# A second column chunk by seven products in a decoder trunk's feed-forward blocks, with two of four weight sums made by accumulating DMA

## The chip, the cores and the metric

The kernel runs on one core of a Trainium2 chip. The metric is the time of one execution in microseconds of device time. The median of three executions of the kernel before is 1845.34 us (1844.8 to 1848.62).

## What is computed

Four decoder layers on 256 tokens of width 1024, all in float32. Each layer has a feed-forward block, a mixer (a short gated convolution, a latent attention, a spatial gating, then the convolution again) and another feed-forward block. The change touches the feed-forward blocks only:

```python
def swiglu(x, w_gate, w_up, w_down):          # w_gate, w_up: 1024 x 2816, w_down: 2816 x 1024
    return (jax.nn.silu(x @ w_gate) * (x @ w_up)) @ w_down

x = x + 0.5 * swiglu(rms_norm(x, norm_g[i, 0]), ffn_gate[i, 0], ffn_up[i, 0], ffn_down[i, 0])
```

There are eight such blocks. The first one is computed plainly in both kernels, so what follows happens seven times.

## The kernel before, in words

**Tiling.** The 256 tokens are two tiles of 128 (t = 0 and t = 1). A float32 product is made of three passes: operand and weight are each split into a high part (`hi`, rounded to the type that TensorE reads) and the rest (`lo`), and hi*hi, hi*lo and lo*hi are added up in PSUM. ScalarE (ACT) makes the high part of a weight unit of 128 x 1024 elements (line 111, tile `whi`), VectorE (DVE) subtracts it from the raw weights (line 122, tile `wlo`), and both token tiles use the pair. The columns of gate and up are cut into chunks of 512 (`FF_CHUNKS`; chunk 5 has 256).

**Turns.** Each token tile is a Python generator (`stream`, `ffn`); one step of it is a turn, which issues about six matmuls with one weight unit (`products`, lines 332, 333, 335). The two tiles take turns alternately (`advance`). The schedule is manual: every engine executes its instructions in the order in which the program issued them.

**Seven products.** For the chunks in `SEVENS` the gate and up products of both token tiles together are computed as a 2 x 2 block product, with the token tiles as the block rows and 256 columns as a block column. Seven block products stand in for eight (Winograd's form of Strassen's scheme). This is the generator `sevens`. It first makes token sums s1 to s4 (the set-up). Then, for each of its units (gate and up of each chunk), it goes through seven products q = 0 to 6. A product is 12 matmuls of 256 columns (line 773 before). Its right operand is one of four weight blocks "11", "12", "21", "22" of 128 x 1024 elements, or a sum of two of them:

```python
right = ("11", "11", "11", "21", "12", "11", "22")
added = (None, "12", "22", None, "22", "21", None)
```

So q = 1, 2, 4 and 5 each need a sum, made in place by DVE (`sum_of`, line 655). Every product's operand goes through `high_of` (ACT, line 631) and `low` (DVE, line 636). Each product is two half-steps of the generator: the first issues drains of earlier products, the next `low` and sums; the second issues the matmuls and the `high_of` two products ahead.

**Order of work.** `beside` decides when the generator moves: at each turn it adds `RATE` half-steps of credit (0.6) and spends whole ones. `block_of` (line 599) loads a block on SP's DMA queue; `load_first` loads the first four during the mixer, and `load` the next unit's four during q = 3, 4 and 5. There are four block buffers, whose names rotate (`next_buffers`): the next unit's "11" goes where "21" was, its "12" where "11" was, its "22" where "12" was, its "21" where "22" was. In the lane of seven products a buffer is thus loaded again when its last `low` is done.

Of the kernel before, what the change touches and what calls it, by code (L numbers as in the profile page):

```python
# [18 lines left out]
ALU = mybir.AluOpType  # L19
# [27 lines left out]
CHAIN_AHEAD = 3  # L47
LAG = 4
CLOSE_AT, CLOSE_LAG = 10, 1
H_READ, H_TAKE, SEVENS_READ = 7, 2, 7  # L50
SEVENS, RATE = (4,), 0.6
SEVENS_TAIL = 10
DOWN_TAIL, OUT_TAIL = 12, 4
X_TURN, X_WRITE, X_READ, X_TAKE = 2, 1, 3, 12
# [112 lines left out]
def program(nc, pools, order, x, positions, norm_g, ffn_gate, ffn_up, ffn_down,  # L167
# [5 lines left out]
    def name(tag):  # L173
        ids[0] += 1
        return f"{tag}_{ids[0]}"

    def slot(shape, dtype=F32):
        return slots.tile(shape, dtype, tag="s", name=name("s"))
# [4 lines left out]
    def acc():  # L183
        return banks.tile([P, 512], F32, tag="bank", name=name("acc"))
# [30 lines left out]
    pause = [0] * NT  # L215
    lag = [LAG]
    lanes = []
    credit = [0.0]
    own = [0] * NT

    def unit(t, m, k, n, c0, width):
# [367 lines left out]
    def next_buffers():  # L589

        buffers.update({"11": buffers["21"], "12": buffers["11"], "22": buffers["12"], "21": buffers["22"]})

    def block_of(i, j, n, m, name_):

        row, col = int(name_[0]) - 1, int(name_[1]) - 1
        c0 = FF_CHUNKS[n][0] + 256 * col
        view = matrices[m][i, j].rearrange("(kt p) n -> p kt n", p=P)[:, 4 * row : 4 * row + 4, c0 : c0 + 256]
        raw = sevens_pool.tile([P, 4, 256], F32, tag=f"block{buffers[name_]}", name=name("block"))
        nc.sync.dma_start(out=raw, in_=view)
        return raw  # L600

    def load_first(i, j, every):
# [8 lines left out]
    def sevens(i, j, chunks, shared, first):  # L611

        (a11, a12), (a21, a22) = lhs[0], lhs[1]
        units = [(n, m) for n in chunks for m in ("gate", "up")]
        raws = [first] + [{} for _ in units[1:]]

        def load(u, *names):
            for name_ in names:
                if u < len(units):
                    raws[u][name_] = block_of(i, j, *units[u], name_)  # L620
# [3 lines left out]
        def combine(x, y, op):  # L624
            f = slot([P, 4, P])
            nc.vector.tensor_tensor(out=f, in0=x, in1=y, op=op)
            return f

        def high(key, src, pool, shape):
            hi, lo = (pool.tile(shape, F32R, tag=tag, name=name(tag)) for tag in ("whi", "wlo")) if pool else (slot(shape, F32R), slot(shape, F32R))  # L630
            nc.scalar.activation(hi, src, AF.Copy)  # L631
            forms[key] = hi, lo, src

        def low(key):
            hi, lo, src = forms[key]
            nc.vector.tensor_tensor(out=lo, in0=src, in1=hi.bitcast(F32), op=ALU.subtract)  # L636
# [3 lines left out]
        def form(key, x, y, op):  # L640
            forms_of_x[key] = combine(x, y, op)
            return forms_of_x[key]

        def high_x(key):
            high(key, forms_of_x[key], None, [P, 4, P])

        right = ("11", "11", "11", "21", "12", "11", "22")
        added = (None, "12", "22", None, "22", "21", None)
        last = 7 * len(units) - 1

        def sum_of(s):
            u, q = divmod(s, 7)
            if s <= last and added[q]:
                to = raws[u][right[q]]
                nc.vector.tensor_tensor(out=to, in0=to, in1=raws[u][added[q]], op=ALU.add)  # L655

        def high_of(s):
            if s <= last:
                high(s, raws[s // 7][right[s % 7]], w_pool, [P, 4, 256])

        s1 = form("s1", a21[2], a22[2], ALU.subtract)
        yield
        s2 = form("s2", s1, a11[2], ALU.subtract)
        high_x("s1")
        high_of(0)
        yield
        low("s1")
        form("s3", a11[2], a21[2], ALU.subtract)
        high_x("s2")
        yield  # L670
        low(0)
        sum_of(1)
        high_x("s3")
        yield
        low("s2")
# [1 line left out]
        high_of(1)  # L677
        yield

        pending = []  # L680
        y = z = x = None
        gates = [None, None]
# [2 lines left out]
        def snapshot(ps):  # L685
            v = slot([P, 256])
            nc.scalar.activation(v, ps[:, :256], AF.Copy)
            return v

        def add(to, ps, v, op):  # L690
            nc.vector.tensor_tensor(out=to, in0=ps[:, :256], in1=v, op=op)
# [42 lines left out]
        for s in range(last + 1):  # L734
            u, q = divmod(s, 7)

            if q == 1:
                v1 = snapshot(y)
            elif q == 3:
                v2 = snapshot(y)  # L740
            elif q == 4:
                vs = [slot([P, 512]) for _ in range(NT)]
                add(vs[0][:, :256], x, v1, ALU.add)
            elif q == 5:
                v3 = snapshot(y)
            elif q == 6:
                add(vs[1][:, 256:], z, v3, ALU.subtract)
            if s + 1 <= last:
                low(s + 1)
            if (s + 2) % 7 in (1, 2):  # L750
                sum_of(s + 2)
            if q == 3:
                next_buffers()
                load(u + 1, "11")
            if q == 4:
                load(u + 1, "12", "22")
            if q == 5:
                load(u + 1, "21")
            if pending:
                pending.pop(0)()  # L760
            yield
            if q == 0:
                y = acc()
            elif q == 1:
                z = acc()
            elif q == 3:
                x = acc()
            ps = (y, z, y, x, y, y, z)[q]
            left = (a11, forms["s1"], forms.get("s2"), a12, forms.get("s3"), a22, forms.get("s4"))
            ah, al, wh, wl = left[q][0], left[q][1], forms[s][0], forms[s][1]  # L770
            for k in range(4):
                for n, (f, w) in enumerate(((ah, wh), (ah, wl), (al, wh))):
                    nc.tensor.matmul(ps[:, :256], lhsT=f[:, k, :], rhs=w[:, k, :], start=q in (0, 1, 3) and k + n == 0, stop=k == 3 and n == 2,  # L773
                                     skip_group_check=True)
            del forms[s]
            high_of(s + 2)
            if (s + 3) % 7 in (4, 5):
                sum_of(s + 3)
            if s == 0:
                low("s3")  # L780
                high_x("s4")
            if s == 1:
                low("s4")
            if q == 6:
                if u % 2 == 0:
                    pending += gate_halves(y, z, v2, vs)
                else:
                    pending += up_halves(y, z, v2, vs, chunks[u // 2], lambda: gates)
            yield
# [494 lines left out]
    def beside():  # L1284
        if not all(half_ is not None for tile_ in lhs for half_ in tile_):
            return
        credit[0] += RATE
        while lanes and credit[0] >= 1:
            credit[0] -= 1
            if next(lanes[0], "end") == "end":  # L1290
                lanes.pop()
                credit[0] = 0.0

    for _ in range(LAG):
        advance(0)
# [33 lines left out]
```

## Time and profile before

| what | value |
|---|---|
| median of three executions | 1845.34 us |
| the profiled execution's own time | 1846.8 us |
| its span, first to last instruction | 1845.1 us |
| instructions | 24822 |
| PE (TensorE matmuls) busy | 1821.9 us, 99% |
| DVE busy | 1286.7 us, 70% |
| ACT busy | 989.3 us, 54% |
| POOL (GpSimd) busy | 146.6 us, 8% |
| HBM read and written | 365.67 MB and 33.03 MB |

The profile comes from one execution. Busy time is the union of an engine's instructions. Matmuls overlap each other by design, so what one costs is read from the distance of two starts and not from its own duration. A DMA's time is counted from its issue to the landing of its last byte.

### The profile page before, as it was taken

The page shows a single profiled execution, that of the slowest core. Times are in us where ns is not written, and L with a number is a line of the kernel's source. Part 1 is how long each engine was busy: PE and PEld are TensorE (multiplying, and loading weights), DVE is VectorE, ACT ScalarE, POOL GpSimd, SP SyncE. Part 2 cuts the span into 40 slices and gives each one's busy share as a digit, 9 for nine tenths or more (in the row PEclk, how much of TensorE's full clock was granted, in tenths as well). Part 3 has the DMA queues.
Part 4 walks back from the last instruction along what each step waited for, and adds up shares of the span by engine and source line. Part 5 has one row for each costly group of instructions (what it writes and reads, how often), then busy time and mean ns, then how long its engine had stood idle before and what let it go on. Part 6 is the DMA issues. An engine that isn't in the chain of part 4 may idle for free.

```text
span 1845.1 us, 24822 instructions
## 1 busy us (share of the span) xinstructions
PE 1821.9 (99%) x9022; PEld 1516.7 (82%) x9022; DVE 1286.7 (70%) x1574; ACT 989.3 (54%) x1422; POOL 146.6 (8%) x279
## 2 busy tenths in 40 slices
PE   8999999999999989999999999999999999999999
PEld 6888887888788868888878888888887888878887
DVE  5556677877687666687668665678667775777773
ACT  5344545554555476554565446565456555546542
POOL 2000101000430142100010001100000000000000
PEclk9999999999999999999999999999999999999999
DMA  7678666669666842676977786657886777665774
GB/s 264 212 244 229 227 213 209 208 195 298 224 217 193 250 154 70 194 226 196 267 238 226 217 262 213 217 176 229 240 262 205 226 233 231 236 204 184 226 235 130
DMA packets 251610, 400.35 MB, mean 217 GB/s; under 512 B 25414, under 2 KB 116448, under 8 KB 251488
## 3 DMA queue, kind: packets, MB, share of 16 engines
q1 hardware_dynamic: 250480, 397.09, 68.7%
q8 instruction: 70, 1.15, 0.3%
q0 software_dynamic: 608, 1.11, 0.2%
q10 hardware_dynamic: 400, 0.57, 0.1%
q14 instruction: 52, 0.43, 0.1%
HBM read 365.67 MB, written 33.03 MB: 216 GB/s over the span
## 4 chain that ended last, share of the span: by engine, by line
PE 91%; DVE 3%; DMA 2%; ACT 2%; issue 1%; SPq 1%; ACTq 0%; DVEq 0%
PE acc L333 27%; PE acc L335 27%; PE acc L332 27%; PE acc L773 8%; DMA xturn<-s 2%; PE tr L298 1%; DVE wlo L122 1%; ACT whi L111 1%; PE acc L1219 1%; PE acc L1192 1%; SPq L467 0%; DMA s<-xturn 0%; DMA raw<-in_ffn_gate_dram 0%; DVE s L814 0%; DVE s L448 0%
## 5 line engine op out<-in xcount | busy, mean ns | idle before, releaser
L332 PE MATMUL acc<-whi,s 128*128 128x512 f32 (+2 forms) x2440 | 937.3, 384 | 4.0 <-ACT whi L111 2.2
L333 PE MATMUL acc<-wlo,s 128*128 128x512 f32 (+2 forms) x2440 | 933.1, 382 | 4.5 <-DVE wlo L122 4.4
L335 PE MATMUL acc<-whi,s 128*128 128x512 f32 (+2 forms) x2440 | 895.8, 382 | 0.0
L122 DVE TENSOR_TENSOR wlo<-raw,whi 128x1024 fp32r<-128x1024 f32 (+1 forms) x580 | 686.7, 1209 | 111.2 <-ACT whi L111 107.8
L111 ACT ACTIVATE whi<-raw 128x1024 fp32r<-128x1024 f32 (+1 forms) x580 | 587.7, 1044 | 90.4 <-DMA raw<-in_ffn_down_dram 41.2
L333 PEld LDWEIGHTS acc<-wlo,s 128*128 128x128 f32 x2440 | 458.8, 188 | 99.2 <-DVE wlo L122 10.6
L335 PEld LDWEIGHTS acc<-whi,s 128*128 128x128 f32 x2440 | 458.7, 188 | 96.5 <-DVE s L291 1.0
L332 PEld LDWEIGHTS acc<-whi,s 128*128 128x128 f32 x2440 | 458.6, 188 | 95.8 <-ACT whi L111 4.3
L773 PE MATMUL acc<-whi,s 128*128 128x256 f32 x784 | 154.4, 280 | 0.0
L631 ACT ACTIVATE whi<-block 128x1024 fp32r<-128x1024 f32 x98 | 103.4, 1056 | 71.0 <-DVE block L655 61.8
L773 PEld LDWEIGHTS acc<-whi,s 128*128 128x128 f32 x784 | 126.8, 188 | 4.0
L522 ACT ACTIVATE s<-acc,evened 128x512 f32<-128x512 f32 (+1 forms) x70 | 44.9, 641 | 143.8 <-PE acc L335 143.7
L291 DVE TENSOR_TENSOR s<-s,s 128x512 fp32r<-128x512 f32 (+1 forms) x58 | 39.9, 689 | 116.4 <-ACT s L290 114.9
L636 DVE TENSOR_TENSOR wlo<-block,whi 128x1024 fp32r<-128x1024 f32 x98 | 118.8, 1212 | 0.4
L410 POOL TENSOR_TENSOR total<-ss,ss 128x1 f32<-128x1 f32 x26 | 8.3, 320 | 1305.9 <-ACT s L401 1305.9
L773 PE MATMUL acc<-wlo,s 128*128 128x256 f32 x392 | 109.8, 280 | 0.0
L324 DVE TENSOR_TENSOR s<-big,s 128x512 fp32r<-128x512 f32 x68 | 46.2, 681 | 79.2 <-ACT s L323 79.2
L401 ACT ACTIVATE s<-x 128x512 bf16<-128x512 f32 x48 | 30.2, 630 | 131.0 <-DVE x L425 96.0
L531 DVE SCALAR_TENSOR_TENSOR s<-acc,evened,s 128x512 f32<-128x512 f32 (+1 forms) x70 | 48.5, 693 | 48.4 <-PE acc L335 48.2
L773 PEld LDWEIGHTS acc<-wlo,s 128*128 128x128 f32 x392 | 73.7, 188 | 4.0
L425 DVE SCALAR_TENSOR_TENSOR x<-acc,x 128x512 f32<-128x512 f32 x32 | 22.1, 689 | 77.8 <-PE acc L335 77.7
L655 DVE TENSOR_TENSOR block<-block,block 128x1024 f32<-128x1024 f32 x56 | 68.5, 1223 | 1.0
(152 smaller groups left out, 900.8 us busy)
## 6 DMA issues: line engine op xcount, KB each, us to landing
raw<-in_ffn_down_dram SPq DMA_DIRECT2D x176, 512.0 KB, 5.9
raw<-in_ffn_gate_dram SPq DMA_DIRECT2D x148, 512.0 KB, 4.8
raw<-in_ffn_up_dram SPq DMA_DIRECT2D x148, 512.0 KB, 4.5
raw<-in_conv_w_in_dram SPq DMA_DIRECT2D x48, 512.0 KB, 5.0
turn<-big SPq DMA_DIRECT2D x32, 512.0 KB, 3.1
big<-turn SPq DMA_DIRECT2D x128, 128.0 KB, 6.0
block<-in_ffn_gate_dram SPq DMA_DIRECT2D x28, 512.0 KB, 6.2
block<-in_ffn_up_dram SPq DMA_DIRECT2D x28, 512.0 KB, 6.3
```

What stands on the lines that cost most here:

```text
L111: self.nc.scalar.activation(hi[:, part], self.loaded[u][:, part], AF.Copy)
L122: self.nc.vector.tensor_tensor(out=lo[:, part], in0=src[:, part], in1=hi[:, part].bitcast(F32), op=ALU.subtract)
L324: nc.vector.tensor_tensor(out=lo.rearrange("p k (i b) -> p k i b", b=32), in0=src, in1=hi.bitcast(F32).rearrange("p k (i b) -> p k i b", b ...
L332: nc.tensor.matmul(ps, lhsT=ah[:, k, :], rhs=wh[:, wk, c], start=first, stop=False)
L333: nc.tensor.matmul(ps, lhsT=ah[:, k, :], rhs=wl[:, wk, c], start=False, stop=False)
L335: nc.tensor.matmul(ps, lhsT=al[:, k, :], rhs=wh[:, wk, c], start=False, stop=last)
L522: nc.scalar.activation(sg[n], ps[:, :w], AF.Silu, scale=r)
L531: nc.vector.scalar_tensor_tensor(out=h, in0=ps[:, :w], scalar=r, in1=sg[n], op0=ALU.mult, op1=ALU.mult)
L631: nc.scalar.activation(hi, src, AF.Copy)
L636: nc.vector.tensor_tensor(out=lo, in0=src, in1=hi.bitcast(F32), op=ALU.subtract)
L655: nc.vector.tensor_tensor(out=to, in0=to, in1=raws[u][added[q]], op=ALU.add)
L773: nc.tensor.matmul(ps[:, :256], lhsT=f[:, k, :], rhs=w[:, k, :], start=q in (0, 1, 3) and k + n == 0, stop=k == 3 and n == 2, skip_group_c ...
```

## The change

`SEVENS` becomes (3, 4): a second chunk of 512 columns goes through seven products, so that four units (28 products) run in each of the seven feed-forward blocks, where two units (14 products) did. The lane moves at 0.8 half-steps a turn in its set-up, which has three more empty half-steps, and at 1.5 from its first product on. All block loads are issued from GpSimd (POOL). The sums for q = 4 and q = 5 are no longer DVE instructions. POOL issues a DMA that reads the second block from HBM once more and adds it onto the first in its buffer. The drain that frees PSUM for q = 6 is issued right behind the product of q = 5, and the turned halves are read back 5 turns ahead of their use where it was 7.

```diff
-H_READ, H_TAKE, SEVENS_READ = 7, 2, 7
-SEVENS, RATE = (4,), 0.6
+H_READ, H_TAKE, SEVENS_READ = 7, 2, 5
+SEVENS, RATE, SETUP_RATE = (3, 4), 1.5, 0.8
...
-    def block_of(i, j, n, m, name_):
+    def block_of(i, j, n, m, name_, onto=None):
...
+        if onto is not None:
+            nc.gpsimd.dma_start(out=onto, in_=view, accum_op=ALU.add)
+            return onto
         raw = sevens_pool.tile([P, 4, 256], F32, tag=f"block{buffers[name_]}", name=name("block"))
-        nc.sync.dma_start(out=raw, in_=view)
+        nc.gpsimd.dma_start(out=raw, in_=view)
...
         def sum_of(s):
             u, q = divmod(s, 7)
-            if s <= last and added[q]:
-                to = raws[u][right[q]]
+            if s > last:
+                return
+            to = raws[u][right[q]]
+            if q in (4, 5):
+                block_of(i, j, *units[u], added[q], to)
+            else:
                 nc.vector.tensor_tensor(out=to, in0=to, in1=raws[u][added[q]], op=ALU.add)
...
         sum_of(1)
+        sum_of(4)
...
+        started[0] = True
...
-            elif q == 6:
-                add(vs[1][:, 256:], z, v3, ALU.subtract)
             if s + 1 <= last:
                 low(s + 1)
             if (s + 2) % 7 in (1, 2):
                 sum_of(s + 2)
+            if (s + 2) % 7 == 1:
+                sum_of(s + 5)
+            if (s + 2) % 7 == 3:
+                sum_of(s + 4)
...
             del forms[s]
+            if q == 5:
+                add(vs[1][:, 256:], z, v3, ALU.subtract)
             high_of(s + 2)
-            if (s + 3) % 7 in (4, 5):
-                sum_of(s + 3)
...
-        credit[0] += RATE
+        credit[0] += RATE if started[0] else SETUP_RATE
```

Three places show what moves. The first is POOL's queue in the second feed-forward block, which held no DMA there before (the block loads stood in SP's queue). The buffers of the second unit are block_375 ("11"), block_381 ("12"), block_382 ("22") and block_386 ("21"); those of the third are block_409, 415, 416 and 421. L602 is a plain load, L599 an accumulating one.

```order
L602 DMA block_375_2983<-in_ffn_up_dram 128x4x256 [waits DMASW6_49,DMASW4_49,DVE_49]
L602 DMA block_381_3014<-in_ffn_up_dram 128x4x256 [waits DMASW5_49,DMASW3_49,DVE_49]
L602 DMA block_382_3016<-in_ffn_up_dram 128x4x256 [waits DMASW2_49]
L602 DMA block_386_3054<-in_ffn_up_dram 128x4x256 [waits DMASW7_49,DMASW1_49,DVE_49]
L599 DMA block_381_3014<-in_ffn_up_dram 128x4x256 [waits DMASW5_49,DVE_49]
L599 DMA block_375_2983<-in_ffn_up_dram 128x4x256 [waits DVE_49]
L602 DMA block_409_3217<-in_ffn_gate_dram 128x4x256 [waits DMASW7_49,DVE_49]
L602 DMA block_415_3257<-in_ffn_gate_dram 128x4x256 [waits DMASW1_49,DVE_49]
```

Six DMAs a unit now stand in one queue, and nearly each waits for DVE to have read a buffer.

The second place is DVE in the second unit of the kernel before, from the `low` of q = 2 (wlo_407) to the sum for q = 5 (block_381 with block_394). Between them stand the sum for q = 4 (block_389) and the `low` of q = 3 (wlo_415); L122 is the plain weights' work, L691 a drain.

```order
L636 TENSOR_TENSOR wlo_407_3281<-block_381_3038,whi_406_3280 128x1024 [waits Activation_49]
L691 TENSOR_TENSOR s_387_3085<-acc_369_2945,s_380_3035 128x256
L122 TENSOR_TENSOR wlo125_3302<-raw125_3127,whi125_3301 128x1024 [waits DMAHW6_49,Activation_49]
L655 TENSOR_TENSOR block_389_3089<-block_389_3089,block_390_3091 128x1024
L122 TENSOR_TENSOR wlo126_3338<-raw126_3152,whi126_3337 128x1024 [waits DMAHW0_49,Activation_49]
L636 TENSOR_TENSOR wlo_415_3334<-block_394_3138,whi_414_3333 128x1024 [waits DMAHW7_49]
L655 TENSOR_TENSOR block_381_3038<-block_381_3038,block_394_3138 128x1024 [waits DVE_49]
```

Both L655 rows have left DVE at this place.

The third place is DVE in the changed kernel, from the `low` of q = 5 of the second unit (wlo_412, the last reader of block_375) to the sum for q = 2 of the third (block_409 with block_416).

```order
L639 TENSOR_TENSOR wlo_412_3242<-block_375_2983,whi_411_3241 128x1024 [waits DMASW1_49,Activation_49]
L639 TENSOR_TENSOR wlo_418_3274<-block_382_3016,whi_417_3273 128x1024 [waits Activation_49]
L122 TENSOR_TENSOR wlo120_3277<-raw120_2986,whi120_3276 128x1024 [waits DMAHW0_49,DVE_49,Activation_49]
L703 TENSOR_TENSOR s_414_3254<-acc_403_3162,s_420_3287 128x256 [waits Activation_49]
L639 TENSOR_TENSOR wlo_424_3317<-block_409_3217,whi_423_3316 128x1024 [waits DMASW2_49,Activation_49]
L662 TENSOR_TENSOR block_409_3217<-block_409_3217,block_415_3257 128x1024 [waits DMASW3_49,DVE_49]
L122 TENSOR_TENSOR wlo121_3324<-raw121_3043,whi121_3323 128x1024 [waits DMAHW1_49,PE_49,Activation_49]
L639 TENSOR_TENSOR wlo_427_3345<-block_409_3217,whi_426_3344 128x1024 [waits PE_49,Activation_49]
L662 TENSOR_TENSOR block_409_3217<-block_409_3217,block_416_3259 128x1024 [waits DMASW4_49,DVE_49]
```

The load of block_415 is issued behind wlo_412, whose buffer it takes over, and the first L662, four DVE instructions later, waits for it.

## Rows read from the trace of the kernel before

**Rows 1.** The page: busy times, and the chain that ended last, by engine.
```profile
PE 1821.9 (99%) x9022; PEld 1516.7 (82%) x9022; DVE 1286.7 (70%) x1574; ACT 989.3 (54%) x1422; POOL 146.6 (8%) x279
...
PE 91%; DVE 3%; DMA 2%; ACT 2%; issue 1%; SPq 1%; ACTq 0%; DVEq 0%
```
**Rows 2.** Timeline of PE: start us, us, engine, line, operation, count.
```profile
324.64 0.28 PE L773 MATMUL acc<-whi,s 128*128 128x256 f32 x1
...
326.06 0.39 PE L332 MATMUL acc<-whi,s 128*128 128x512 f32 x1
...
331.64 0.28 PE L773 MATMUL acc<-whi,s 128*128 128x256 f32 x1
```
**Rows 3.** Stretches: us; busy of PE, PEld, DVE, ACT, POOL; clock, DMA share, GB/s.
```profile
324.60:405.80 81.20, 81.20 (x451) 70.15 (x450) 62.87 (x66) 41.35 (x51) 0.00 (x0) 1.00 0.70 211
...
1691.30:1772.30 81.00, 81.00 (x451) 70.09 (x450) 62.74 (x66) 41.36 (x51) 0.00 (x0) 1.00 0.69 212
```
**Rows 4.** Timeline of DVE, then of ACT, in the first lane of seven products.
```profile
327.29 1.23 DVE L655 TENSOR_TENSOR block<-block,block 128x1024 f32<-128x1024 f32 x1
...
334.56 1.22 DVE L122 TENSOR_TENSOR wlo<-raw,whi 128x1024 fp32r<-128x1024 f32 x1
...
337.97 1.22 DVE L655 TENSOR_TENSOR block<-block,block 128x1024 f32<-128x1024 f32 x1
...
328.55 1.06 ACT L631 ACTIVATE whi<-block 128x1024 fp32r<-128x1024 f32 x1 [3.02 <-DVE block L655]
```
**Rows 5.** Groups by line from 324.6 to 405.8 us: count, busy us, mean ns, idle before.
```profile
L122 DVE TENSOR_TENSOR wlo<-raw,whi 128x1024 fp32r<-128x1024 f32 x23 | 27.7, 1215 | 9.6 <-ACT whi L111 9.6
...
L636 DVE TENSOR_TENSOR wlo<-block,whi 128x1024 fp32r<-128x1024 f32 x13 | 15.7, 1211 | 0.1
...
L631 ACT ACTIVATE whi<-block 128x1024 fp32r<-128x1024 f32 x12 | 12.7, 1055 | 8.7 <-DVE block L655 7.2 <-PE acc L773 1.5
L655 DVE TENSOR_TENSOR block<-block,block 128x1024 f32<-128x1024 f32 x7 | 8.6, 1222 | 0.1
L531 DVE SCALAR_TENSOR_TENSOR s<-acc,evened,s 128x512 f32<-128x512 f32 x7 | 5.2, 749 | 7.5 <-PE acc L335 7.5
L533 DVE STREAM_TRANSPOSE big<-s 128x512 f32<-128x512 f32 x7 | 5.0, 712 | 0.2
...
L687 ACT ACTIVATE s<-acc 128x256 f32<-128x256 f32 x6 | 2.3, 380 | 13.6 <-PE acc L773 13.6
L691 DVE TENSOR_TENSOR s<-acc,s 128x256 f32<-128x256 f32 x5 | 2.1, 411 | 0.0
```
**Rows 6.** Stretches again: DVE nearly full, and the time of POOL's loads.
```profile
494.70:534.70 40.00, 40.00 (x204) 33.76 (x203) 38.34 (x41) 23.55 (x31) 28.95 (x47) 1.00 0.71 238
1021.00:1027.00 6.00, 6.00 (x34) 5.13 (x33) 5.75 (x8) 4.70 (x6) 2.76 (x4) 1.00 0.69 191
```
**Rows 7.** DMA issues: queue, count, KB each, median us from issue to landing.
```profile
block<-in_ffn_gate_dram SPq DMA_DIRECT2D x28, 512.0 KB, 6.2
block<-in_ffn_up_dram SPq DMA_DIRECT2D x28, 512.0 KB, 6.3
...
turn<-s SPq DMA_DIRECT2D x14, 256.0 KB, 4.3
s<-turn SPq DMA_DIRECT2D x56, 64.0 KB, 4.3
...
s<-in_sg_v_norm_dram POOLq DMA_DIRECT2D x2, 256.0 KB, 5.2
s<-in_sg_w_s_dram POOLq DMA_DIRECT2D x2, 256.0 KB, 5.4
```
**Rows 8.** Timeline of POOL: its own loads, the nearest to what the change issues.
```profile
1021.12 0.69 POOL L858 DMA_DIRECT2D s<-in_sg_v_norm_dram  x1 [67.70 <-DMA raw<-in_ffn_up_dram]
...
1025.03 0.75 POOL L861 DMA_DIRECT2D s<-in_sg_w_s_dram  x1 [0.60 <-DVE s L691]
```
**Rows 9.** DMA traffic in 40 slices of the stretch 324.6 to 405.8 us.
```profile
GB/s 246 6 0 144 161 219 233 211 125 269 382 272 344 320 377 381 352 130 236 51 207 99 159 132 127 99 214 203 162 243 119 63 331 224 284 239 151 278 369 276
```

More of the change, by code (lines that the diff above doesn't have):

```diff
@@ L217, in program @@
     lanes = []
-    credit = [0.0]
+    credit, started = [0.0], [False]
     own = [0] * NT
@@ L662, in sevens @@
         yield
+        yield
         s2 = form("s2", s1, a11[2], ALU.subtract)
@@ L665, in sevens @@
         high_of(0)
+        yield
         yield
@@ L670, in sevens @@
         yield
+        yield
         low(0)
         sum_of(1)
+        sum_of(4)
         high_x("s3")
@@ L1291, in beside @@
                 lanes.pop()
-                credit[0] = 0.0
+                credit[0], started[0] = 0.0, False
     for _ in range(LAG):
```

## The prediction

> **What bounds the kernel now.** I read the page first, then the chain of waits, then the timeline of PE, then the stretches in which the seven products run, and last the DMAs. The page says that PE is busy for 1821.9 of 1845.1 us, and the chain that ended last is PE for 91% [rows 1]. A busy PE need not be a full one, so the timeline has to say whether matmuls follow each other without gaps. They do: twelve matmuls of 256 columns, one product, take from 324.64 to 326.06, which is 1.42 us, and the 24 of 512 columns behind them take 5.58 us, which is 0.2325 us each [rows 2]. In the lane of seven products PE is busy for 81.20 of 81.20 us in the first block and 81.00 of 81.00 in the last of seven [rows 3]. So the kernel is bound by PE's work, and taking matmuls away pays in full as long as the other engines deliver their operands in time. In the lane DVE has 62.87 us of work in 81.20, and the DMA engines are busy for 0.70 of it [rows 3]. These two are what the change leans on.
>
> **PE: what is removed and added.** A chunk of 512 columns done plainly costs, for gate and up, two token tiles, eight row blocks and three passes, 96 matmuls of 512 columns: 96 x 0.2325 = 22.32 us. Done by seven products it costs 14 products: 14 x 1.42 = 19.88 us [rows 2]. The difference is 2.44 us a block, and 7 x 2.44 = 17.1 us in all. All of it lies on the path that sets the end.
>
> **The lane's new pace.** A unit of seven products is 14 half-steps. At 1.5 a turn that is 9.33 turns of six plain matmuls, 9.33 x 1.395 = 13.02 us, and 7 x 1.42 = 9.94 us of products: 22.96 us a unit, 1.64 us a half-step (before, at 0.6, it was 42.5 us and 3.03 us). Four units take 91.8 us. Everything that products need of DVE, ACT and the DMAs now has about half the time it had.
>
> **DVE.** By the order of the changed kernel the lane holds 28 `low`, 18 plain `wlo` and 8 sums of 1024 columns. In a row without waits these start 3.41 / 3 = 1.14 us apart [rows 4], so 54 x 1.14 = 61.6 us. Beside them stand 5 drains with their transposes, 5 x (0.74 + 0.71) = 7.3 us, 10 drains of seven products at 0.41 [rows 5], 4.1 us, and 15 smaller instructions at about 0.6 by my estimate from the same rows, 9 us. That is 82 us in 91.8, or 89%, where it was 77%. Without moving two sums a unit to the DMA it would be 8 x 1.14 = 9.1 us more, 99%. DVE at 89% need not stop PE: from 494.7 to 534.7 it was busy for 38.34 of 40.00 us and PE for all 40.00 [rows 6]. I cost it at nothing. The cover is the few microseconds by which a `low` stands ahead of its product, three half-steps or 4.9 us less the 1.2 us it takes itself.
>
> **The chain through the new DMAs.** This is where the sign is decided. Within a unit the work now forms a ring. The block "12" of the next unit takes the buffer of "11", so its load waits for the `low` of q = 5. The load (L) is followed by the DVE sum for q = 1, ACT's high part and `low`, then the sum for q = 2, high part and `low`. Then comes the accumulating DMA (A) onto the same buffer, then the high part and `low` of q = 5, and the ring closes. Its part on the engines is 2 x (1.22 + 1.06 + 1.21) + 1.06 + 1.21 = 9.25 us [rows 4, 5]. ACT began 0.03 us after DVE's sum had ended (328.55 against 327.29 + 1.23) [rows 4]. With seven such steps and a plain `wlo` that fills each gap on DVE I take 9.6 us.
>
> For L the nearest rows are POOL's own loads of 256 KB, 5.2 and 5.4 us, which are half as large, and the same blocks of 512 KB on SP's queue, 6.2 and 6.3 us, which stand behind other weights there [rows 7]. I take 5.9, between them. For A no row exists. It can't be below a plain load, 5.9 us; above, I bound it by two loads one after the other, 11.8 us. It is nearest to the plain load, since HBM gives the same bytes and what is added is a reading of the buffer on the chip. I add one more pass of 0.524 MB at the 337 GB/s that the DMA engines held over eight slices from 269 to 352 [rows 9], 1.6 us, and get 7.5 us. The ring then takes 5.9 + 7.5 + 9.6 = 23.0 us against 22.96 us of PE work. There is something in hand besides: the matmuls of q = 5 stand nine half-steps, 14.8 us, behind the `low` of q = 2, and A, high part and `low` need 9.9 of these, which leaves 4.9 us. A block has three turns of the ring, so its stall is 3 x (L + A + 9.6 - 22.96) - (14.8 - A - 2.4), if that is positive. With these values it is not: 0.1 less 4.9. At L = 5.9 a stall begins at A = 8.7 us, and at A = 9.3 it eats the whole 2.44 us.
>
> The Trainium skill ("DMA: Bandwidth & Descriptors", the anatomy of one DMA on the gpsimd path) puts such a DMA at about 2.0 us and its bytes over 436 GB/s. By that L would be an estimated 3.2 us and no stall would come near. POOL's loads at 5.2 and 5.4 us for half the bytes [rows 7] speak against so short a time here, and I keep to the rows.
>
> **What else moves.** The extra readings are 28 units x 2 x 0.524 = 29 MB. In the lane 20 block transfers, some 20 plain ones and about 2 MB of turned halves are 23 MB in 91.8 us, 250 GB/s where it was 211 [rows 3]; the plain weights are loaded up to six units ahead, which is the cover. A copy of PSUM by ACT ahead of q = 5 now has one turn, 1.395 us, between the products of q = 4 and q = 5 at the tightest. It takes 0.38 us [rows 5] and may stand behind a 1.06 us high part; I put 1.5 us on this for all 28 units, between nothing and 28 x 0.2 = 5.6 us. The issue of a DMA holds POOL for 0.69 to 0.75 us [rows 8], and nothing on POOL is due in the lane. The block loads leave SP's queue, where they cost 28 x 2 issues that hid under its waits; that gives nothing. Halves read back 5 turns ahead have three turns of each tile, six in all, 8.4 us, for a reading of 4.3 us [rows 7]; the writing stands further ahead. If that cover went, a late half would hold PE by its lateness once a block. The set-up at 0.8 only fills the turns in which DVE was free.
>
> **The sum.** 17.1 - 1.5 = 15.6 us less. Against the profiled execution, 1846.8 us with 1.7 us around its span, that is 1831.2; it lay 1.5 us over the median, so I forecast **1830 us**. A measurement of this kernel tells about 0.2%, 3.7 us, from no change.
>
> **The rivals.**
> - *The accumulating DMA is slow, and the ring becomes the bound.* Price: at A = 10.5 us, in the upper half of the bounds, 3 x 3.04 - 1.9 = 7.2 us a block, 50 us in all, so 1845.3 - 17.1 + 50 = 1879 us; at 11.8 it is 1915. It decides from A = 9.3 us. For it: the DMA engines will be busier than at 0.70, and the same blocks took 6.2 to 6.3 us on SP's queue. Against it: POOL's loads came at 5.2 to 5.4 us with the DMA engines at 0.69 [rows 6, 7].
> - *DVE can't be filled to 89%.* If its 18.3 us of idle time a lane (81.20 less 62.87) [rows 3] came on top of 82 us, a lane would take 100.3 us, 8.5 more than PE's 91.8, and the kernel 1888 us. The 40 us at 96% [rows 6] speak against it.
> - *POOL's DMA issue waits for DVE.* If each issue waited for one DVE instruction of 1.2 us, L and A would be 7.1 and 8.7 us and the stall 3 x 2.44 - 3.7 = 3.6 us a block: 1845.3 - 17.1 + 25.4 = 1854 us. POOL's four loads held it for 2.76 us together, 0.69 each, while DVE was busy for 5.75 of 6.00 us [rows 6], which speaks against it. The rule behind this is the Trainium skill's ("SBUF — State Buffer", "SBUF: two separate sides"): descriptors of a DMA issued from GpSimd can't be written while DVE holds the shared port.
> - *Gain and stalls cancel,* with A between 8.8 and 9.4 us: 1842 to 1849 us.
>
> **How the numbers follow.** The forecast gets 0.58, since two estimated latencies decide it with some 1.2 us in hand on A. The slow accumulation gets 0.19, DVE 0.07, POOL's issue 0.05, the cancelling case 0.11. So faster 0.58, the same 0.11, slower 0.31. The likeliest case alone reaches from 1826 (no loss at the copies, and a little from SP's queue) to 1841. The range of 8 in 10 takes in the cancelling case, POOL's issue and the slow accumulation up to A = 10.5: 1825 to 1880.
>
> **What would show it.** Right: about 17 us less on the sum of PE's matmuls, a lane of some 92 us with PE busy throughout and DVE at about 89%, accumulating DMAs landing in 7 to 8 us, and ACT's high part of q = 5 waiting for them at most briefly. Wrong: PE idle in the lane ahead of product q = 5 or q = 1, with DVE or ACT waiting for a block's DMA; landings over 9 us; a lane longer than 94 us; or POOL's issues stretched far beyond 0.75 us.

## The result, and the profile after

The changed kernel takes 1868.41 us (median of four runs, 1867.01 to 1870.15) where the kernel before took 1845.72 beside it: a ratio of 1.0118, 95% interval 1.0101 to 1.0134. I had forecast 1830 us. The range of 1825 to 1880 held the time; the sign was wrong.

The page of the changed kernel, as in [rows 1]:

```profile
span 1868.4 us, 26191 instructions
...
PE 1822.2 (98%) x9526; PEld 1538.7 (82%) x9526; DVE 1353.3 (72%) x1665; ACT 1036.9 (55%) x1513; POOL 299.4 (16%) x447
...
PE 45%; DMA 6%; issue 6%; DVE 4%; ACT 2%; POOL 1%; DVEq 0%; ACTq 0%; POOLq 0%
```

PE's busy time hasn't fallen, and DMAs, which had 2% of the chain, now have 6% (the shares named add up to 64% of the span here, so that the rest of the chain isn't told). The lanes of seven products, as in [rows 3] (us; busy of PE, PEld, DVE, ACT, POOL; clock, DMA share, GB/s); the first, the fifth and the last of seven:

```profile
326.20:420.00 93.80, 91.04 (x601) 82.50 (x600) 79.26 (x88) 58.20 (x78) 21.16 (x23) 1.00 0.94 255
...
1244.60:1343.70 99.10, 94.45 (x600) 84.77 (x599) 80.31 (x90) 59.98 (x79) 21.63 (x24) 0.97 0.89 241
...
1713.60:1808.40 94.80, 91.25 (x601) 82.44 (x600) 79.17 (x88) 58.71 (x78) 18.19 (x19) 1.00 0.94 253
```

They take 93.8 to 99.1 us, not 91.8, and PE idles in them. DVE has its 79 to 80 us of work, about what I had counted, and the traffic is the 250 GB/s I had counted, but the DMA engines stand at 0.94.

To split the time I took the distance from each matmul's start to the next over the whole trace. What 512 columns (0.232 us), 256 (0.118) and the smaller shapes need is work, a distance of about twice that I call doubled, and the rest is gaps. The work went from 1804.0 to 1786.9 us, 17.1 less. Doubled distances went from 2.9 to 14.0, and gaps from 18.9 to 47.9. Together with 1.3 us of small delays that is 24.3 more; the spans differ by 23.3. So the gain is there in full, and gaps (29 us) and doubled distances (11 us) took it more than twice over. Most of the doubled distances are matmuls at half clock: the trace's granted clock stands at 0.5 for two stretches of 3.41 us in the kernel before and for eight in the changed one, and the matmuls in them took 2.9 and 12.3 us more than they need. The rest are short waits.

The gaps have one main place: 14 stalls of 0.3 to 2.9 us ahead of product q = 5, mostly in the second and third unit of a lane, 24.5 us together (ahead of experiments 1 and 2 I call them 1.6 to 2.9 us; two are of 0.3 and 0.8). The second unit of the second lane: the `low` of q = 2 on DVE, then POOL, ACT, DVE and PE in turn (L599 is the accumulating DMA, L699 the PSUM copy):

```profile
539.74 1.23 DVE L639 TENSOR_TENSOR wlo<-block,whi 128x1024 fp32r<-128x1024 f32 x1
...
541.27 1.29 POOL L599 DMA_DIRECT2D block<-in_ffn_up_dram  x1 [6.03 <-DVE wlo L639]
...
549.28 2.01 ACT L634 ACTIVATE whi<-block 128x1024 fp32r<-128x1024 f32 x2 [3.56 <-DMA block<-in_ffn_up_dram]
551.20 1.04 ACT L111 ACTIVATE whi<-raw 128x1024 fp32r<-128x1024 f32 x1
552.14 0.67 ACT L522 ACTIVATE s<-acc,evened 128x512 f32<-128x512 f32 x1
552.71 0.37 ACT L699 ACTIVATE s<-acc 128x256 f32<-128x256 f32 x1
...
550.38 2.36 DVE L639 TENSOR_TENSOR wlo<-block,whi 128x1024 fp32r<-128x1024 f32 x2 [3.06 <-ACT whi L634]
...
551.14 0.40 PE L335 MATMUL acc<-whi,s 128*128 128x512 f32 x1
553.13 0.39 PE L787 MATMUL acc<-whi,s 128*128 128x256 f32 x1 [1.59 <-ACT s L699]
```

The DMA is issued at 541.27, 0.3 us after the `low` of q = 2 has ended (540.97), and lands 7.9 us later. ACT has waited 3.56 us for it. The high part of q = 5 ends at 550.3 and its `low` at 551.6, 0.2 us after PE arrives (551.37). But PE also needs the copy, and that stands behind the high part of q = 6, a plain high part and a drain: 553.08. Two causes are mixed here, a block that comes at the last moment and a copy stuck behind it in ACT's queue.

The longer of these stalls cost twice. PE around a stall of 2.88 us:

```profile
575.62 0.28 PE L335 MATMUL acc<-whi,s 128*128 128x256 f32 x1
578.62 0.58 PE L787 MATMUL acc<-whi,s 128*128 128x256 f32 x1 [2.72 <-ACT s L699]
...
581.35 0.41 PE L332 MATMUL acc<-whi,s 128*128 128x256 f32 x1
...
583.09 0.28 PE L787 MATMUL acc<-whi,s 128*128 128x256 f32 x1
```

The product from 578.62 takes 2.73 us instead of 1.42. The trace shows granted clock 0.5 there (1.2 GHz) for 3.4 us, and there are five such stretches in the lanes, each behind an idle PE of 1.96 to 2.88 us.

The page's DMA issues, as in [rows 7]:

```profile
block<-in_ffn_gate_dram POOLq DMA_DIRECT2D x84, 512.0 KB, 7.2
block<-in_ffn_up_dram POOLq DMA_DIRECT2D x84, 512.0 KB, 6.5
```

### The profile page after: what moved, and what is told of

Its sections match the earlier page's. It is cut to its first block, busy times and chain, and to the rows that moved or that the text cites. A ratio compares the mean times of both kernels' runs of the same rounds, so it can differ in the third digit from the quotient of the medians.

```text
span 1868.4 us, 26191 instructions
## 1 busy us (share of the span) xinstructions
PE 1822.2 (98%) x9526; PEld 1538.7 (82%) x9526; DVE 1353.3 (72%) x1665; ACT 1036.9 (55%) x1513; POOL 299.4 (16%) x447
## 3 DMA queue, kind: packets, MB, share of 16 engines
q0 software_dynamic: 46304, 89.21, 20.4%
## 4 chain that ended last, share of the span: by engine, by line
PE 45%; DMA 6%; issue 6%; DVE 4%; ACT 2%; POOL 1%; DVEq 0%; ACTq 0%; POOLq 0%
PE acc L333 12%; PE acc L332 12%; PE acc L335 12%; PE acc L787 6%; DMA block<-in_ffn_gate_dram 4%; DMA block<-in_ffn_up_dram 2%; PE tr L298 1%; DVE wlo L122 1%; POOL block L599 1%; DVE block L662 1%; DVE wlo L639 1%; PE acc L1233 1%; PE acc L1206 1%; ACT whi L111 0%; DVE s L531 0%
## 5 line engine op out<-in xcount | busy, mean ns | idle before, releaser
L332 PE MATMUL acc<-whi,s 128*128 128x512 f32 (+3 forms) x2216 | 851.9, 384 | 4.7 <-ACT whi L111 3.0
L333 PE MATMUL acc<-wlo,s 128*128 128x512 f32 (+3 forms) x2216 | 846.8, 382 | 2.4 <-DVE wlo L122 2.4
L335 PE MATMUL acc<-whi,s 128*128 128x512 f32 (+3 forms) x2216 | 809.9, 382 | 0.0
L122 DVE TENSOR_TENSOR wlo<-raw,whi 128x1024 fp32r<-128x1024 f32 (+2 forms) x524 | 622.0, 1210 | 52.8 <-ACT whi L111 52.5
L111 ACT ACTIVATE whi<-raw 128x1024 fp32r<-128x1024 f32 (+2 forms) x524 | 530.0, 1042 | 78.5 <-DMA raw<-in_ffn_down_dram 48.5
L335 PEld LDWEIGHTS acc<-whi,s 128*128 128x128 f32 x2216 | 418.6, 189 | 87.3 <-DVE s L291 1.0
L332 PEld LDWEIGHTS acc<-whi,s 128*128 128x128 f32 x2216 | 418.7, 189 | 83.5 <-ACT whi L111 4.2
L634 ACT ACTIVATE whi<-block 128x1024 fp32r<-128x1024 f32 x196 | 205.3, 1055 | 274.9 <-DVE block L662 161.3
L787 PE MATMUL acc<-whi,s 128*128 128x256 f32 x1568 | 315.9, 284 | 22.3 <-ACT s L699 22.2
L639 DVE TENSOR_TENSOR wlo<-block,whi 128x1024 fp32r<-128x1024 f32 x196 | 237.1, 1216 | 68.5 <-ACT whi L634 67.4
L787 PEld LDWEIGHTS acc<-whi,s 128*128 128x128 f32 x1568 | 256.2, 190 | 36.8 <-ACT s L699 29.5
L787 PE MATMUL acc<-wlo,s 128*128 128x256 f32 x784 | 222.4, 284 | 4.5 <-DVE wlo L639 4.5
L599 POOL DMA_DIRECT2D block<-in_ffn_gate_dram x28 | 36.6, 1307 | 274.5 <-DVE block L662 195.6
L662 DVE TENSOR_TENSOR block<-block,block 128x1024 f32<-128x1024 f32 x56 | 68.6, 1225 | 7.9 <-DMA block<-in_ffn_gate_dram 5.8
L602 POOL DMA_DIRECT2D block<-in_ffn_up_dram x56 | 42.5, 761 | 144.3 <-DVE wlo L639 144.3
```

The lines of the kernel that those rows point to most:

```text
L111: self.nc.scalar.activation(hi[:, part], self.loaded[u][:, part], AF.Copy)
L122: self.nc.vector.tensor_tensor(out=lo[:, part], in0=src[:, part], in1=hi[:, part].bitcast(F32), op=ALU.subtract)
L332: nc.tensor.matmul(ps, lhsT=ah[:, k, :], rhs=wh[:, wk, c], start=first, stop=False)
L333: nc.tensor.matmul(ps, lhsT=ah[:, k, :], rhs=wl[:, wk, c], start=False, stop=False)
L335: nc.tensor.matmul(ps, lhsT=al[:, k, :], rhs=wh[:, wk, c], start=False, stop=last)
L599: nc.gpsimd.dma_start(out=onto, in_=view, accum_op=ALU.add)
```

## The experiments

Ratios are to the kernel before, on the same chip; gaps and doubled distances are split as above, in the profiled execution. That execution lies within 3.1 us of the median beside it but for three: all sums on DVE (5.0 above), sum of q = 4 on DVE (4.0 below), and q = 5 on DVE with five buffers (7.7 above). Two kernels, adding left out and q = 5 on DVE with loads on SyncE, have no stretch at half clock while PE works, so their 4.6 and 4.8 us are short waits alone.

| kernel | us | ratio, 95% interval | gaps | doubled |
|---|---|---|---|---|
| before | 1845 to 1846 | 1 | 18.9 | 2.9 |
| the change | 1868.4 | 1.0118 (1.0101 to 1.0134) | 47.9 | 14.0 |
| adding left out | 1834.9 | 0.9948 (0.9935 to 0.9962) | 22.2 | 4.6 |
| sum of q = 5 on DVE | 1841.3 | 0.9974 (0.9964 to 0.9985) | 29.1 | 5.2 |
| sum of q = 4 on DVE | 1849.3 | 1.0021 (1.0012 to 1.0030) | 30.3 | 7.7 |
| all sums on DVE | 1860.5 | 1.0083 (1.0067 to 1.0099) | 49.7 | 7.4 |
| loads on SyncE | 1856.6 | 1.0053 (1.0036 to 1.0070) | 41.0 | 10.6 |
| copy and high part moved | 1882.5 | 1.0200 (1.0181 to 1.0220) | 57.0 | 16.6 |
| copy alone ahead | 1862.4 | 1.0090 (1.0073 to 1.0106) | 45.1 | 7.0 |
| five buffers | 1864.7 | 1.0094 (1.0075 to 1.0112) | 44.2 | 10.3 |
| one chunk | 1859.0 | 1.0073 (1.0057 to 1.0088) | 29.9 | 5.4 |
| q = 5 on DVE, five buffers | 1837.5 | 0.9956 (0.9941 to 0.9972) | 31.4 | 5.4 |
| q = 5 on DVE, loads on SyncE | 1838.3 | 0.9957 (0.9944 to 0.9970) | 24.2 | 4.8 |
| the same, `low` of q = 1 early | 1846.4 | 1.0006 (0.9998 to 1.0015) | 32.0 | 6.2 |

**1. ScalarE's order.** My first theory was the copy's place.

```diff
-            elif q == 5:
-                v3 = snapshot(y)
-            if s + 1 <= last:
+            if q == 5:
+                low(s)
+            if s + 1 <= last and q != 4:
                 low(s + 1)
...
-            high_of(s + 2)
+            if q == 4:
+                v3 = snapshot(y)
+                high_of(s + 1)
+            if q != 3:
+                high_of(s + 2)
```

> ScalarE's order alone is changed: the PSUM copy that product q=5 needs is issued right behind product q=4 and ahead of the high part of q=5, and the low part of q=5 right ahead of its product. The accumulating DMA and all loads stay. Theory 'copy stuck in ScalarE's queue' (the copy stands behind a high part that waits for the accumulating DMA): of the 14 stalls of 1.6 to 2.9 us ahead of q=5 (24 us together) some 0.5 us each is left, and most of the 11 us of half clock that follows them goes; 1868 falls to 1840 to 1850. Rival 'the block itself is late' (high and low part end too late whatever stands between): the stalls stay over 1.3 us each, 1862 to 1870. Rival 'the pace': the wait moves to another product of the unit, 1855 to 1870.

Measured: 1882.5, slower than either theory allowed. What ended PE's weight loads' waits shows why (us in total, times, longest), the change first, then this kernel:

```profile
PEld acc L787 <- ACT s L699: 29.5, 21, 2.9
PEld acc L787 <- DVE wlo L639: 7.5, 10, 0.8
```

```profile
PEld acc L787 <- DVE wlo L639: 38.2, 34, 2.7
PEld acc L787 <- ACT whi L634: 11.1, 23, 1.4
```

The copy no longer ends a wait, but my edit also put the high part of q = 5 behind product q = 4, so that now `low` ends them, 1.14 us also in every first and last unit, where the change had stalls in two of 14. The edit was no clean test: it brought a wait of its own.

**2. The copy alone.** The same lines, with only the copy moved:

```diff
-            elif q == 5:
-                v3 = snapshot(y)
...
+            if q == 4:
+                v3 = snapshot(y)
             high_of(s + 2)
```

> Only the PSUM copy that product q=5 needs moves: in ScalarE's queue it stands ahead of the high part of q=6 and of the plain high part and drain behind it, but still behind the high part of q=5, which waits for the accumulating DMA. In the changed kernel the copy ends 3.5 us after the high part of q=5 begins (549.28 to 553.08 us). If the copy's place is what costs, the 14 stalls of 1.6 to 2.9 us fall by 1 to 1.7 us each and the half clock behind them with them: 1842 to 1854. If the block itself is late (its low part ends 2.3 us after the landing), less than 5 us is gained: 1863 to 1869.

Measured: 1862.4, some 6 us less, just below what the late block would give; the intervals of the two kernels touch. The stalls in the second unit fell to 0.8 us or less where they had stood at 1.6 to 2.1, but others of 1.2 us came in the third. Gaps fell by only 2.8 us. Doubled distances fell by 7.0: the stalls are shorter, and one stretch at half clock is left in the lanes where there were five. So the copy's place is a small part, and the block is late by itself.

**3. Is it the adding?**

```diff
-            nc.gpsimd.dma_start(out=onto, in_=view, accum_op=ALU.add)
+            nc.gpsimd.dma_start(out=onto, in_=view)
```

> The 56 accumulating DMAs become plain ones: the same bytes, queue and waits, but the block is written over and not added to, so the sums of q=4 and q=5 are left out. If the adding is what makes them long (issue 1.30 us against 0.76, landing 7.9 against 6.6 in the changed kernel), the block of q=5 comes 1.3 to 1.8 us sooner, most of the stalls ahead of it and of their half clock go: 1842 to 1855. If a plain transfer in that place is as slow (two or three transfers of 512 KB in flight together), 1862 to 1870.

Measured: 1834.9, 33.5 us less, and 10 below the kernel before. That is faster than the theory of the adding had it (1842 to 1855). The stalls ahead of q = 5 are gone, and so is the half clock. The first lane, as in the rows of lanes above:

```profile
326.30:417.30 91.00, 90.52 (x600) 82.54 (x599) 79.08 (x88) 58.72 (x77) 17.16 (x23) 1.00 0.83 263
```

L599 in the changed kernel, then with plain transfers (duration ns min/median/max):

```profile
L599 POOL DMA_DIRECT2D block<-in_ffn_gate_dram x28: 1277/1302/1352, 324.0 to 1766.7; - x28
...
DMA to landing us min/median/max: 5.8/7.9/11.1
```

```profile
L599 POOL DMA_DIRECT2D block<-in_ffn_gate_dram x28: 748/748/822, 324.1 to 1732.0; - x28
...
DMA to landing us min/median/max: 4.2/4.6/5.9
```

GpSimd's queue on the page (packets, MB, share of 16 engines), the change first:

```profile
q0 software_dynamic: 46304, 89.21, 20.4%
```

```profile
q0 software_dynamic: 24800, 89.21, 16.0%
```

The same bytes go in 21504 more packets, 384 for each of the 56 DMAs: in the traces an adding DMA moves in 512 packets of 1 KB, the plain one in its place in 128 of 4 KB. The issue takes 0.55 us longer and the landing 3.3 us (medians). The engines' time grew as well: 20.4% of 16 engines over 1868.4 us less 16.0% over 1832.3 is 1408 engine-us, or 1.6 us of all 16 engines for each adding DMA. Landings issue by issue show where it hurts. Medians over the seven lanes, adding, for units 1 to 4: 6.1, 9.3, 9.0 and 6.2 us for q = 4; 6.3, 8.0, 9.6 and 6.0 us for q = 5. Plain ones land within 5.9 us in all four. The DMA engines in the first lane, from the issue to the landing of the first unit's q = 4, of the third unit's q = 5 and of the fourth unit's q = 4 (the share counts packets that overlap each for itself, so that it can pass 1):

```profile
324.00:330.10 6.10, 6.10 (x38) 5.38 (x37) 6.03 (x8) 4.39 (x6) 1.34 (x1) 1.00 0.68 111
...
378.90:388.20 9.30, 9.30 (x57) 8.23 (x57) 8.56 (x11) 2.83 (x4) 2.01 (x2) 1.00 1.10 269
398.50:404.80 6.30, 6.30 (x55) 6.30 (x55) 5.23 (x6) 5.73 (x10) 1.27 (x1) 1.00 1.00 222
```

An adding DMA takes 6 us in the first and the last unit and 8 to 11 us in the two between them, and how busy the engines are doesn't tell the two kinds apart: at 1.00 it lands in 6.3 us. One of the kernel of experiment 7, with no other block in flight, takes 7.9 us from 553.15, with the engines at 0.81:

```profile
553.15:561.00 7.85, 7.85 (x42) 6.62 (x41) 7.71 (x8) 5.12 (x7) 3.89 (x22) 1.00 0.81 161
```

So the adding is what makes these DMAs long; why it makes some 6 us long and others 8 to 11 stays open.

**4. One adding DMA a unit, or none.** The sum of q = 5 goes back to DVE at its old place, then that of q = 4 instead, then both (the edit of the first):

```diff
-            if q in (4, 5):
+            if q == 4:
                 block_of(i, j, *units[u], added[q], to)
...
-            if (s + 2) % 7 == 3:
-                sum_of(s + 4)
...
             high_of(s + 2)
+            if (s + 3) % 7 == 5:
+                sum_of(s + 3)
```

> The sum of q=5 goes back to VectorE, from the block that is already in SBUF; the sum of q=4 stays an accumulating DMA. 28 DMAs of 512 KB fewer, 4 sums of 1.22 us more on VectorE in each lane (87 of 92 us). Both theories that blame the accumulation of q=5 expect the stalls ahead of q=5 gone (24 us, and most of the 11 us of half clock): 1833 to 1845. Rival 'VectorE is full': late low parts at q=1 and q=5, stalls of 0.6 to 2 us, 1850 to 1870. Rival 'loads are late because GpSimd issues them': no change within 6 us of 1868.

> The mirror of the kernel with the sum of q=5 moved: the sum of q=4 goes back to VectorE and q=5 stays an accumulating DMA, loads from GpSimd. Number of DMAs and VectorE's work are the same in both. If the place of q=5 is what costs (10.4 us behind the low part of q=2 for DMA, high and low part), the stalls ahead of q=5 stay: 1855 to 1870. If two accumulations a unit are what is too much, the one left lands in under 7 us and it is as fast as its mirror: 1838 to 1846.

> All four sums on VectorE, no accumulating DMA at all; loads still from GpSimd; pace and chunks as in the change. VectorE has 82 + 8 x 1.22 = 92 us of work in a lane of 92 us. If only the accumulations cost, 1830 to 1845, as with one sum moved. If VectorE then can't fill the pace (my prediction's reason for the DMAs), low parts come late in every unit: lanes of 96 us and more, 1850 to 1885, slower than the kernel with one sum moved.

Measured: 1841.3, 1849.3 and 1860.5. The first lane with q = 5 on DVE, then with all sums there:

```profile
326.00:417.50 91.50, 90.75 (x600) 82.49 (x599) 83.16 (x92) 58.62 (x77) 15.89 (x19) 1.00 0.83 235
```

```profile
326.20:420.00 93.80, 91.46 (x599) 82.50 (x599) 87.62 (x96) 59.52 (x78) 11.90 (x16) 1.00 0.65 207
```

With q = 5 on DVE five of the seven lanes take 91.5 to 91.7 us, the predicted length. With all sums there DVE has 87.62 us in 93.80, the waits are for DVE (most for `low` parts, some for a drain), and the lanes take 93.9 to 97.5 us: DVE can't keep the pace, as the prediction had it. One sum a unit has to leave it, and two adding DMAs a unit cost more than they give. That it should be q = 4 which leaves, the mirror shows: the lone DMA of q = 5 lands in 6.1 us (median), and still the kernel is 8 us slower, with lanes of 92.4 to 93.5 us even in its profiled execution, the fastest of ten. Neither expectation for it held in full.

**5. The queue of the plain loads.** One line, `nc.gpsimd.dma_start` to `nc.sync.dma_start` for the block's load.

> Only the plain loads go back to SyncE's queue, as in the kernel before; the 56 accumulating DMAs stay on GpSimd. Theory 'copy stuck' and rival 'the block is late' expect little: accumulations that leave up to 0.8 us sooner and land a little faster where no load of the same queue is being written, 1855 to 1868. Rival 'loads are late because GpSimd issues them, or its descriptors are slow': 1835 to 1848. A loss is possible where a waiting load on SyncE holds up the layer's own loads: up to 1880.

Measured: 1856.6, 12 us less. That is the lower end of what the late block or the stuck copy would give (1855 to 1868), and far from the rival's 1835 to 1848. Loads land in 5.8 us where they took 6.6 (medians). The stalls of the third unit fall to between nothing and 1.3 us; those of the second stay at 1.8 to 3.3. Whether the earlier landing or GpSimd's shorter queue does it was not told apart.

**6. The ring cut.**

```diff
-    buffers = {"21": 0, "11": 1, "12": 2, "22": 3}
+    buffers = {"21": 0, "11": 1, "12": 2, "22": 3, "spare": 4}
...
-        buffers.update({"11": buffers["21"], "12": buffers["11"], "22": buffers["12"], "21": buffers["22"]})
+        buffers.update({"11": buffers["21"], "12": buffers["spare"], "22": buffers["12"], "21": buffers["22"], "spare": buffers["11"]})
```

> A fifth block buffer (two of 29 small tiles given up for it), so that the next unit's block 12 no longer waits for the low part of q=5: the ring of my prediction is cut, nothing else moves. If the ring carries the lateness of one unit into the next, the loads of 12 go out some 5 to 10 us sooner, the sum of q=1 no longer waits for them and the stalls of the second and third unit shrink: 1845 to 1860. If the delay arises within each unit (low part of q=2, accumulating DMA of 8 to 9.6 us, high part, low part against 10.4 us), no change within 4 us: 1864 to 1872; the two small tiles fewer could only add.

Measured: 1864.7, which the intervals don't separate from the change. The second unit's stalls stay at 1.2 to 2.3 us, so that delay arises within a unit. The third unit's do shrink, from 8 us in all to 1.4, as they would if the ring carried lateness into it, but others of 0.7 to 3.3 us come in first and fourth units. Nor did only the ring move: the loads, which can now leave sooner, land in 8.7 us where they took 6.6 (medians). Cutting the ring, on which my working had turned, gave nothing in all.

**7. The moves alone, at the old pace.** `SEVENS, RATE, SETUP_RATE = (4,), 0.6, 0.6`.

> The change with one chunk by seven products at 0.6 half-steps a turn, as before, so the accumulating DMAs, GpSimd's queue and the other moves alone: 28 accumulating DMAs, a unit of 42.5 us, no second chunk. If the accumulations cost only where the pace leaves them no room, 1841 to 1849, no different from the kernel before. If they cost by themselves (GpSimd's issue, HBM, contention with the weights' loads), 1852 to 1862.

Measured: 1859.0, the price that I had put on the rival, yet not for its reason. Six lanes take 81.2 to 81.3 us, as before. The second takes 95.9, with one stall. POOL, then ACT, then PE:

```profile
553.15 1.30 POOL L599 DMA_DIRECT2D block<-in_ffn_up_dram  x1 [11.71 <-DVE block L662]
...
586.82 0.21 POOL L1028 TENSOR_SCALAR rope<-rope 128x32 f32<-128x32 f32 x1
587.30 1.38 POOL L599 DMA_DIRECT2D block<-in_ffn_up_dram  x1 [0.28 <-issue]
...
593.48 1.06 ACT L634 ACTIVATE whi<-block 128x1024 fp32r<-128x1024 f32 x1 [21.96 <-DMA block<-in_ffn_up_dram]
...
599.01 0.58 PE L787 MATMUL acc<-whi,s 128*128 128x256 f32 x1 [12.16 <-ACT s L699]
```

Between the two L599 POOL prepares tables for the attention, some 33 us of small instructions with one wait for their input, once in the kernel. The DMA for q = 5 stands behind them in its in-order queue, and PE waits 12.16 us. Elsewhere the DMAs cost nothing at this pace.

**8. Towards a better kernel.** The sum of q = 5 on DVE, with loads on SyncE; with five buffers; and the first again with the `low` of q = 1 issued at the end of q = 6.

> Both edits that helped: sum of q=5 on VectorE, plain loads on SyncE; 28 accumulating DMAs for q=4 alone on GpSimd. If the two gains have separate causes (the accumulation of q=5, and loads that land sooner), they add in part: 1832 to 1839. If the loads only helped through the accumulation of q=5, it equals the kernel with the sum of q=5 moved: 1839 to 1843.

> Sum of q=5 on VectorE, and the fifth buffer (two of 29 small tiles given up); loads from GpSimd. What is left of stalls there is 0.65 us at q=2 and 0.45 us at the first product of a unit, both for a low part that VectorE makes late. If a late block 12 is behind them, they go: 1833 to 1838. If it is VectorE's full queue, nothing changes: 1839 to 1843, or more if small tiles run short.

> The best so far (sum of q=5 on VectorE, loads on SyncE: 1838) with the low part of q=1 issued half a product sooner, ahead of a drain for which VectorE waits 2.8 us with nothing else to do. Left there were stalls of 0.65 us at q=2 of some ten units and of 0.45 us further on, 7 to 9 us in all. If VectorE's order makes them, 1829 to 1835. If VectorE then waits for the high part of q=1 instead and the drain comes late, no gain or up to 6 us more: 1836 to 1844.

Measured: 1838.3, 1837.5 and 1846.4. The first two beat both kernels by 0.4% (before) and 1.6% (the change); their intervals overlap with each other and with that of the sum of q = 5 on DVE alone. In the kernel with loads on SyncE five of seven lanes take 91.4 to 91.5 us. With five buffers the time is what a late block 12 would give, yet not for that reason as far as the trace tells: the waits that were to go are still there in every lane, 0.6 to 0.7 us in the second unit and 0.4 to 0.5 in the third. By the order of the products they stand at q = 1, for a `low`, and at q = 6, for a drain, and not at q = 2 and at the first product, as I had written.

The third edit failed. In each lane it moved one `low` on DVE, in the third unit; in the second, where the wait at q = 1 stands, DVE's order stayed as it was and so did the wait. Whether an earlier `low` would help there is thus not shown. In the third unit a 0.43 us stall grew to 1.2 us, for a drain that DVE now does later:

```profile
392.23 0.38 PE L785 MATMUL acc<-whi,s 128*128 128x256 f32 x1 [1.02 <-DVE s L703]
```

## Why the prediction was wrong, point by point

- **PE's saving** was right: 17.1 us predicted, 17.1 measured as matmul time.
- **The pace** was right: 91.8 us a lane predicted; with the adding left out five of the seven lanes take 90.9 to 91.0, with one wait of 0.6 to 0.7 us in each.
- **DVE** was counted well (82 us, measured 79 to 80), and it does fail with all sums. To cost it at nothing was too little: with the adding left out, nine waits of 0.6 to 0.9 us for a `low` remain, seven of them at q = 1 of the second unit, 6.2 us in all.
- **The step that failed is the chain through the new DMAs,** in two terms. The first is A as one number. The 7.5 us are close to the median of 7.9, but I built A on "one more pass" of bytes and let it be the same for every unit. It is 6 us in the first and the last unit and 8 to 10 in the two between. In the third, at 9.6, it passes the 8.7 at which I had stalls begin; in the second, at 8.0, it doesn't, and PE stalls there in every lane. L was a little short as well, 6.6 us (median) and not 5.9. I had counted bytes (250 GB/s, measured 241 to 255) and not the engines' time: 0.70 x 250 / 211 would be 0.83, which the kernel without the adding shows (0.83), and the change had 0.94. What makes A differ between the units stays open.
- The second is the cover: q = 5 "nine half-steps, 14.8 us, behind the `low` of q = 2", of which 4.9 us were to be left over. I let that `low` run as early as it is issued. It runs when the two sums ahead of it and the work between them are through, and ends at 540.97 in the unit shown, 10.4 us ahead of PE's arrival at 551.37. Over all 28 units the trace gives 9.9 to 13.7 us (medians 10.0, 10.4, 12.1 and 10.4 for units 1 to 4). With A, high part and `low` at 10.3 nothing is left. The ring itself, my formula's first part, did not decide: cutting it left the time as it was (experiment 6).
- **ACT's copy,** put at 1.5 us and at most 5.6: moving it alone gave 6 us. I had seen it behind one high part, not behind a high part that waits for the DMA and three instructions more.
- **TensorE's clock** had no term at all. Half clock cost 12.3 us where it had cost 2.9. Five of the eight stretches stand in the lanes, each behind a stall, 7.6 us in all; the other three stand outside the lanes, where the kernel before had its two.
- **GpSimd's queue:** "nothing on POOL is due" was wrong for the issue itself, 1.30 us and not 0.75, and in one lane of experiment 7. That loads leave SyncE "gives nothing" was wrong too; putting them back gave 12 us.
- **The rivals.** The slow accumulation, at 0.19, was right in the cause and not in the path. It had the mechanism through the ring and a price of 50 us at an A of 10.5, and by its own formula the measured median of 7.9 gives no stall; the gaps came to 29 us and the half clock to 9. The cancelling case has a slip: by my formula 1842 to 1849 us belong to an A of 9.2 to 9.4, and 8.8 gives 1831. The rival in which POOL's issue waits for DVE is not borne out: all 56 issues took 1.28 to 1.35 us with DVE busy for 85% of the lane. The rule that stood behind it (the Trainium skill, "SBUF — State Buffer", "SBUF: two separate sides") shows in no issue of any run here: plain ones from GpSimd took 0.75 to 0.90 us, adding ones 1.25 to 1.40.
- The Trainium skill's 2.0 us and bytes over 436 GB/s ("DMA: Bandwidth & Descriptors", the anatomy of one DMA on the gpsimd path) gave an estimated 3.2 us for a block. No run reached it: the quickest plain one from GpSimd landed in 4.1, and those that stood in the place of the adding ones in 4.6 (median).

## What to carry to other kernels

Moving work from a full engine to the DMAs is priced in DMA-engine time and in landing times measured in that very place, not in bytes; where a DMA of a new kind is planned, one run with the plain kind in its place tells what the kind costs. The slack ahead of a consumer is counted from when the producer's queue really gets to it, and every instruction queued behind the one that waits belongs to the price. A long stall on a full TensorE can cost more than itself: in the change each of the five of 1.96 us and more was followed by some 1.5 us lost at half clock.

## What the hardware showed that I had not expected

- An accumulating DMA of 512 KB from GpSimd, 128 rows of four pieces of 1 KB, moves in 512 packets of 1 KB where the plain one has 128 of 4 KB, holds GpSimd for 1.30 us against 0.75, takes 1.6 us more of all 16 engines, and lands in 5.8 to 11.1 us. A plain one in the same place landed in 4.2 to 5.9. The share of busy engines did not tell a quick landing from a slow one (6.3 us at 1.00, 7.9 us at 0.81).
- In the change half clock followed the five stalls of 1.96 to 2.88 us in the lanes, and lasted 3.4 us each time. It does not follow every long stall: with five buffers, stalls of 2.26, 2.33 and 3.28 us had none behind them.
